# One level of Strassen's scheme in the input products of four SwiGLU layers, with two of the weight sums made by accumulating transfers

## The chip, the core and the metric

The program runs on one core of one Trainium2 chip. The metric is the device time of one execution in microseconds. A core has TensorE (PE), which multiplies a stationary operand of up to 128x128 with a moving one; VectorE (DVE), ScalarE (ACT) and GpSimd (POOL) for the elementwise work; SyncE (SP), which here issues the transfers; and 16 DMA engines. PSUM holds the accumulators of PE, eight banks of 128x512 float32.

## The reference

A trunk of two layers, 512 tokens, width 1024, in float32:

```python
def swiglu(h, w_in, w_out):
    gu = h @ w_in
    a, b = gu[..., :D_FF], gu[..., D_FF:]
    return (jax.nn.silu(a) * b) @ w_out

for l in range(DEPTH):
    x = x + 0.5 * swiglu(rmsnorm(x, norm_ffn1[l]), w_ffn1_in[l], w_ffn1_out[l])
    h = rmsnorm(x, norm_mix[l])
    x = x + mixing_sublayer(h, w_in[l], b_forget[l], ret_norm[l], w_o_ret[l], w_o_fox[l], w_out[l])
    x = x + 0.5 * swiglu(rmsnorm(x, norm_ffn2[l]), w_ffn2_in[l], w_ffn2_out[l])
return rmsnorm(x, norm_final)
```

D_FF is 2816, so each of the four `w_in` has 1024 rows and 5632 columns, 2816 for the gate and 2816 for the up half, 22 tiles of 128 columns each. `mixing_sublayer` (retention, forgetting attention, gates) is not touched by the change but for the buffers that it shares.

## The kernel before

The residual stream lives on chip as eight tiles `x0` to `x7`, features on the partitions and 512 tokens along the free axis. Products are made to float32 accuracy from operands that are rounded to PE's float32r: every operand is split into a rounded part H (a cast on ACT) and the rest L (a subtract on DVE or POOL), and each product is three matmuls, H by H, H by L and L by H (`mm3`, lines L175 to L177; in `proj_tok`, with tokens standing, L194 to L196).

A SwiGLU (`ffn`) runs in two parts of 12 and 10 column tiles (`FF_PARTS`). `ffn_in` takes two tiles of the gate, then two of the up half: `pair` loads a 1 MiB block of weights (`staged`, two staging buffers named `wst`), and `split` makes H and L of each 128x1024 half, in a ring of three buffers `wH` and three `wL`. The weights stand and the tokens move: 8 row tiles by 3 matmuls of 512 columns per column tile, 1056 for an FFN. The result has features on the partitions. DVE multiplies it by R, the inverse norm of every token spread over the partitions (it goes through DRAM for that); ACT makes the silu, POOL the product `u` (L284) and its L part. The output product follows for the part: 24 or 20 blocks of `w_ffn_out`, and DVE adds the result to the residual tile (L324). In the second part `prep` makes H and L of each finished residual tile for the next stage, and its square for the norm. The last SwiGLU (`ffn_last`) makes its output product with tokens standing, and ends with the final norm.

At the start, token tiles `xi` are loaded and turned by PE (`xT`, L825), and 256 KB pieces of the first weights come between them, so that the first product can begin with the first token tile.

A scheduler of the language orders the instructions of each engine and gives them buffers; every engine then runs its list in order. All loads are issued by SP and lie in one queue, in the order of SP's list.

Of the kernel before, what the change touches and what calls it, by code (L numbers as in the profile page):

```python
# [22 lines left out]
FF_PARTS = ((0, 12), (12, 10))  # L23
# [10 lines left out]
    "x": 8, "xh": 16, "v": 8, "o": 8, "y": 8, "g": 6, "r": 3, "qk": 8, "a": 8, "p": 3, "t": 5,  # L34
}
WB = 3
# [3 lines left out]
def trunk(  # L40
# [36 lines left out]

    def wide(name, dt=F32):
        return sp.tile([P, 10 * P], dt, tag="wide", bufs=3, name=name)
# [13 lines left out]
    # ---- constants  # L93
# [3 lines left out]
    gvec = const.tile([P, P], F32, name="gvec")  # L97
    G.memset(gvec, 0.0)
    load(gvec[0:DEPTH * KD], norm_ffn1.rearrange("l (m p) -> (l m) p", p=P))
    gcol = const.tile([P, P], F32, name="gcol")  # L100
    ones = const.tile([P, P], F32, name="ones")
# [5 lines left out]
    # per-feature gains, one column of 128 features each  # L107
    def gain(n, l, m):
        c = (n * DEPTH + l) * KD + m
        return gcol[:, c:c + 1]  # L110

# [4 lines left out]
    def gains(a, b):  # L116
        o = pst("pt", 2, "gT")
        PE.transpose(o[:, 0:P], gvec, ident)
        V.tensor_copy(gcol[:, a:b], o[:, a:b])

    def rest_of_constants():
        for n, v in ((1, norm_mix), (2, norm_ffn2)):
            load(
                gvec[n * DEPTH * KD:(n + 1) * DEPTH * KD, :],
                v.rearrange("l (m p) -> (l m) p", p=P),
            )
        load(gvec[6 * KD:NV, :], ret_norm.rearrange("l (m p) -> (l m) p", p=P))
        gains(DEPTH * KD, NV)
        load(mask, c_mask)
# [5 lines left out]
    # ---- weights: a float32 chunk, split into a rounded part and the rest  # L135
# [7 lines left out]
    def halves(nm, dims, idx):  # L143
        """a pair [128, *dims] of float32r tiles for each index of the loaded chunk"""
# [21 lines left out]
    def pair(nm, parts, nk=KD):  # L166
        """columns of two output tiles: for each, H and L as [128, nk, 128]"""
# [11 lines left out]
    def proj(o, w, mvH, mvL, k0=0, nk=KD, first=True, last=True):  # L179
        """o[128 features, T] (+)= W[:, 128 columns].T @ x over nk row tiles."""  # L180
# [7 lines left out]
    def proj_tok(o, b, w, k0, nk, last_k, mvH, mvL):  # L188
        """o[tokens of block b, 512 columns] += x.T @ W over nk row tiles"""
# [8 lines left out]
    # ---- residual tile done: operands of the next sublayer and its statistics  # L198
    def prep(n, l, m, src=None):
        g = gain(n, l, m)  # L200
        src = xs[m] if src is None else src
        xH[m], xL[m] = st("xh", f"xH{m}", FR), st("xh", f"xL{m}", FR)
# [5 lines left out]
        sq = st("a", f"sq{m}")  # L208
        S.activation(sq, src, AF.Square)  # L209
        if m == 0:  # L210
            sqa[0] = sq
        else:
# [687 lines left out]
```

## Time and profile before

| | us |
|---|---|
| median of 3 runs | 2246.72 (2246.62 to 2247.15) |
| span of the profiled execution | 2244.8 |
| PE busy | 2229.5 (99 %) |
| DVE busy | 1058.3 (47 %) |
| ACT busy | 773.7 (34 %) |
| POOL busy | 579.8 (26 %) |
| chain that ended last | 99 % PE |
| DMA queue of SP | 217.36 MB, 30.6 % of 16 engines |

The busy time of an engine is the time in which at least one of its instructions runs; matmuls overlap each other, so that one shows a duration of 0.39 us where the next starts 0.23 us later. The chain of waits follows the last instruction back to what released it, step by step. Idle time of an engine matters only where that engine, or one that waits for it, is on this chain.

### The profile page before, as it was taken

The numbers are of one execution on the slowest core, as the hardware profiler recorded it, in microseconds if no ns is written. First come the engines' busy times: TensorE is split into PE (matmuls) and PEld (weight loads), VectorE is DVE, ScalarE is ACT, GpSimd is POOL, SyncE is SP. The second block draws the span as 40 slices with busy tenths as digits, with TensorE's granted clock in tenths as the row PEclk, the third lists the DMA queues.
The fourth block names the chain that finished last, engine by engine and source line by source line (L and its number), as shares of the span: only waits on it lengthen the run. The fifth ranks groups of instructions, "written<-read, shape, count | busy, mean of one in ns | idle before, by whom it ended". The sixth has DMA issues, their size and how long they took to land.

```text
span 2244.8 us, 25332 instructions
## 1 busy us (share of the span) xinstructions
PE 2229.5 (99%) x10142; PEld 1850.5 (82%) x10142; DVE 1058.3 (47%) x1452; ACT 773.7 (34%) x1136; POOL 579.8 (26%) x419
## 2 busy tenths in 40 slices
PE   9999999999999999999999999999999999999998
PEld 7888888888878888888888888888888788888887
DVE  4433444557754444344434334446487544433442
ACT  4322233345542332222333223334455333232232
POOL 3220321454221232012232101225532222220121
PEclk9999999999999999999999999999999999999999
DMA  5323224333222332322332232243332233322231
GB/s 159 103 80 117 94 78 125 94 88 115 78 78 94 104 106 81 106 96 80 108 105 98 89 108 94 82 129 90 104 99 76 75 99 118 98 95 94 94 108 61
DMA packets 221557, 218.97 MB, mean 98 GB/s; under 512 B 7040, under 2 KB 205040, under 8 KB 221440
## 3 DMA queue, kind: packets, MB, share of 16 engines
q1 hardware_dynamic: 221440, 217.36, 30.6%
q8 instruction: 79, 1.29, 0.2%
q14 instruction: 38, 0.31, 0.0%
HBM read 215.18 MB, written 2.16 MB: 97 GB/s over the span
## 4 chain that ended last, share of the span: by engine, by line
PE 99%; DVE 0%; SPq 0%; DMA 0%; ACT 0%; issue 0%; POOLq 0%; POOL 0%; ACTq 0%
PE pb L177 7%; PE pb L175 7%; PE pb L176 7%; PE pa L177 7%; PE pa L175 7%; PE pa L176 7%; PE po L176 6%; PE po L177 6%; PE po L175 6%; PE pg L177 3%; PE pg L176 3%; PE pg L175 3%; PE pv L196 1%; PE prq L175 1%; PE pv L195 1%; PE prq L177 1%
## 5 line engine op out<-in xcount | busy, mean ns | idle before, releaser
L284 POOL TENSOR_TENSOR u<-t,sil 128x512 f32<-128x512 f32 x88 | 128.5, 1462 | 876.5 <-DVE t L282 169.8
L175 PE MATMUL po<-uH,wH_o 128*128 128x512 f32 x528 | 205.4, 389 | 0.0
L176 PE MATMUL po<-uL,wH_o 128*128 128x512 f32 x528 | 205.4, 389 | 0.0
L177 PE MATMUL po<-uH,wL_o 128*128 128x512 f32 x528 | 205.4, 389 | 0.0
L282 DVE TENSOR_TENSOR t<-pb,R 128x512 f32<-128x512 f32 x88 | 60.8, 691 | 237.3 <-PE pb L177 236.1
L273 DVE TENSOR_TENSOR t<-pa,R 128x512 f32<-128x512 f32 x88 | 60.5, 691 | 231.8 <-PE pa L177 224.8
L137 ACT CAST wH_o<-wst_o 128x768 fp32r<-128x768 f32 (+1 forms) x96 | 75.3, 785 | 245.4 <-PE po L176 176.9
L138 POOL TENSOR_TENSOR uL<-u,uH 128x512 fp32r<-128x512 f32 x88 | 127.7, 1452 | 62.3 <-ACT uH L137 62.3
L138 DVE TENSOR_TENSOR wL_o<-wst_o,wH_o 128x768 fp32r<-128x768 f32 (+1 forms) x96 | 87.1, 907 | 109.9 <-ACT wH_o L137 100.5
L213 POOL TENSOR_TENSOR sq<-sq,sq 128x512 f32<-128x512 f32 x42 | 65.7, 1565 | 203.8 <-ACT sq L209 203.7
L176 PEld LDWEIGHTS po<-uL,wH_o 128*128 128x128 f32 x528 | 99.1, 188 | 20.8
L177 PEld LDWEIGHTS po<-uH,wL_o 128*128 128x128 f32 x528 | 99.1, 188 | 20.5
L175 PEld LDWEIGHTS po<-uH,wH_o 128*128 128x128 f32 x528 | 99.1, 188 | 20.5
L177 PE MATMUL pg<-xH,wL_g 128*128 128x512 f32 x256 | 100.5, 393 | 0.0
L176 PE MATMUL pg<-xL,wH_g 128*128 128x512 f32 x256 | 100.4, 392 | 0.0
L175 PE MATMUL pg<-xH,wH_g 128*128 128x512 f32 x256 | 100.4, 392 | 0.0
L137 ACT CAST uH<-u 128x512 fp32r<-128x512 f32 x88 | 54.7, 622 | 124.3 <-POOL u L284 124.2
L324 DVE SCALAR_TENSOR_TENSOR x<-po,x 128x512 f32<-128x512 f32 x48 | 33.2, 692 | 90.9 <-PE po L177 90.9
L177 PE MATMUL pa<-xH,wL_f20a 128*128 128x512 f32 x176 | 68.6, 390 | 0.0
L177 PE MATMUL pa<-xH,wL_f11a 128*128 128x512 f32 x176 | 68.6, 390 | 0.0
L177 PE MATMUL pa<-xH,wL_f21a 128*128 128x512 f32 x176 | 68.6, 390 | 0.0
L177 PE MATMUL pb<-xH,wL_f21b 128*128 128x512 f32 x176 | 68.6, 390 | 0.0
(306 smaller groups left out, 6011.8 us busy)
## 6 DMA issues: line engine op xcount, KB each, us to landing
wst_o<-in_w_ffn_out SPq DMA_DIRECT2D x24, 768.0 KB
wst_g<-in_w_in SPq DMA_DIRECT2D x16, 1024.0 KB
wst_o<-in_w_ffn_out SPq DMA_DIRECT2D x24, 640.0 KB
wst_f20a<-in_w_ffn_in SPq DMA_DIRECT2D x11, 1024.0 KB
wst_f20b<-in_w_ffn_in SPq DMA_DIRECT2D x11, 1024.0 KB
wst_f11a<-in_w_ffn_in SPq DMA_DIRECT2D x11, 1024.0 KB
wst_f11b<-in_w_ffn_in SPq DMA_DIRECT2D x11, 1024.0 KB
wst_f21a<-in_w_ffn_in SPq DMA_DIRECT2D x11, 1024.0 KB
```

Source lines behind the costliest of these rows:

```text
L137: S.copy(hi, src)
L138: (lo_eng or V).tensor_tensor(out=lo, in0=src, in1=hi.bitcast(F32), op=ALU.subtract)
L175: PE.matmul(o, wh, mh, start=first, stop=False)
L176: PE.matmul(o, wh, ml, start=False, stop=False)
L177: PE.matmul(o, wl, mh, start=False, stop=last)
L195: PE.matmul(o, mvH[kk][:, bs], lo[:, k], start=False, stop=False)
L196: PE.matmul(o, mvL[kk][:, bs], h[:, k], start=False, stop=kk == last_k)
L213: G.tensor_tensor(out=sqa[0], in0=sqa[0], in1=sq, op=ALU.add)
L273: V.tensor_tensor(out=t, in0=o, in1=R(), op=ALU.mult)
L282: V.tensor_tensor(out=t, in0=o, in1=R(), op=ALU.mult)
L284: G.tensor_tensor(out=u, in0=t, in1=sil[jj], op=ALU.mult)
L324: V.scalar_tensor_tensor(out=xs[m], in0=os_[jj], scalar=0.5, in1=xs[m], op0=ALU.mult, op1=ALU.add,)
```

## The change

Strassen's scheme, in Winograd's form, splits a product of two matrices into quarters and makes seven products of quarters for eight. Here the tokens are cut into two halves of 256, the 1024 rows of the weights into two halves of 512, and the columns into gate and up. Of a group of column tiles the four weight blocks are A11 and A12 (the gate's upper and lower rows) and, of the up half, S1's first summand (upper rows) and A22 (lower rows). Line by line:

- `FF_PARTS` names three parts of two groups; a group has four column tiles, but one of each FFN has two.
- `prep_forms` takes the place of `prep` ahead of an FFN. From residual tiles k and k+4 it makes the seven forms of the tokens: scaled tiles (`b2`, `n1`), and four sums `m1` to `m4` of half tiles, each split into H and L.
- `ffn_group` loads seven blocks of 512 rows: A12, A11 and A22 plainly; S1 (the sum of the up half's upper and lower rows) and S3 (the sum of the gate's and the up half's upper rows) each by a plain load of one summand and a second transfer, issued by POOL, that adds the other to it in the buffer (`summed`). Two more sums, S1+A11 and S1+A11+A12, are made by DVE (`more`). The buffers swap roles between even and odd groups. Seven steps follow, each 24 matmuls in which a 128-token form stands and 512 columns of weights move (256 in the group of two tiles).
- The accumulators now have tokens on the partitions: the norm is a scalar per partition, `u` is made by ACT and DVE, and `turned` brings it back by 22 x 4 transposes per FFN, for the output product.
- Weight rings get a fourth place from the tag `y`. Output blocks are 1 MiB (768 KB in the last part). `ffn` may finish residual tiles in pairs (k, k+4).
- At the start all token tiles are loaded first, in the order 4, 0 (the loop over `i` starts at tile 4, and `prep_forms` runs from tile 0 on).

```diff
-FF_PARTS = ((0, 12), (12, 10))
+FF_PARTS = (((0, 4), (4, 4)), ((8, 4), (12, 4)), ((16, 2), (18, 4)))
...
+    def prep_forms(n, l, k, stat=True):
...
+        scaled(b2[:, 0:T], b2[:, T:2 * T], x2, gain(n, l, k + 4))
...
+        scaled(n1[:, 0:H2], n1[:, H2:T], x1[:, 0:H2], ngain(n, l, k))
+        b1 = st("t", "b1")
+        S.activation(b1, x1, AF.Copy, scale=gain(n, l, k))
...
+        V.tensor_tensor(out=m1, in0=b1[:, 0:H2], in1=b1[:, H2:T], op=ALU.subtract)
...
+        split(mt, mh, ml)
...
+            square(x1, k == 0)
+            square(x2, False)
...
+    def wtile(w, i):
+
+        tag = w if i % 4 else "y"
...
+        def summed(ts, r0, c0, r1, c1):
+            for s, t in enumerate(ts):
+                load(v3(t), piece(r0, c0, s))
+                G.dma_start(v3(t), piece(r1, c1, s), accum_op=ALU.add)
+            return ts
+
+        K2 = 4 * P
+        raw = {}
+        raw["A12"] = plain(small_tiles("qk", "A12_") if odd else big_tile("A12_"), K2, ca)
+        raw["A11"] = plain(small_tiles("qk", "A11_") if odd else big_tile("A11_"), 0, ca)
+        raw["S1"] = summed(small_tiles("v", "S1_"), 0, cb, K2, cb)
+        raw["S3"] = summed(small_tiles("v", "S3_"), 0, ca, 0, cb)
+        raw["A22"] = plain(big_tile("A22_") if odd else small_tiles("qk", "A22_"), K2, cb)
...
+        def step(nm, form, banks, first):
+            wh = weights(nm)
+            for q in range(2):
+                o = banks[q][:, 0:cw]
+                for k in range(4):
+                    h, lo = (x[:, k % nk] for x in wh[k // nk])
+                    sh, sl = forms[form, k, q]
+                    mm(o, sh, h, start=first and k == 0, stop=False)
+                    mm(o, sh, lo, start=False, stop=False)
+                    mm(o, sl, h, start=False, stop=k == 3)
...
+        Y = [acc("Y0"), pst("po", 1, "Y1")]
+        step("A12", "b21", Y, True)
+        X = [acc("X0"), acc("X1")]
+        step("A11", "n11", X, True)
...
+            S.copy(c1[q], X[q][:, 0:cw])
+            V.tensor_tensor(out=c1[q], in0=Y[q][:, 0:cw], in1=c1[q], op=ALU.subtract)
+            S.activation(c1[q], c1[q], AF.Silu, scale=r[:, q:q + 1])
+        more("S1", "A11", "A11")
+        step("S1A11", "m2", X, False)
...
+        step("S1", "m1", W, True)
+        step("S3", "m3", X, False)
...
+        more("S1A11", "A12", "A12")
+        step("S1A11A12", "b22", W, False)
...
+        step("A22", "m4", X, False)
...
+    def turned(ub, j, u):
+
+        o = pst("pt", 2, "uT")
+        for b in range(TB):
+            PE.transpose(o[:, b * P:(b + 1) * P], ub[b][:, j * P:(j + 1) * P], ident)
...
-        if m % 2 == 0:
-            first_weights(m // 2)
...
+        if m < 4:
+            prep_forms(0, 0, m)
```

The order of the instructions shows the change at three places. First ACT at the start of the program. `w0H` is a cast of a 256 KB weight piece, `xH` the token tile's rounded part, `sq` a square. Before:

```order
L137 CAST w0H_98<-w0_96 128x512
L203 ACTIVATE xH0_113<-xT_108,gcol_77 128x512
L137 CAST w0H_104<-w0_102 128x512
L209 ACTIVATE sq0_117<-xT_108 128x512
L137 CAST w0H_139<-w0_137 128x512
L203 ACTIVATE xH1_127<-xT_122,gcol_77 128x512
L137 CAST w0H_145<-w0_143 128x512
```

And now, from its 20th operation on, up to the cast that PE's first product waits for (`wH_0`, from A12's first half; `mh` are casts of the four sums):

```order
L152 CAST wH_2_307<-wst_A11_0_252 128x1024
L152 CAST mh0_149<-mt_144 128x1024
L152 CAST wH_3_311<-wst_A11_0_252 128x1024
L152 CAST mh2_209<-mt_204 128x1024
L244 ACTIVATE b2_1_166<-x5_86,gcol_74 128x512
L152 CAST mh1_178<-mt_173 128x1024
L244 ACTIVATE b2_3_227<-x7_88,gcol_74 128x512
L244 ACTIVATE b2_2_196<-x6_87,gcol_74 128x512
L152 CAST mh3_239<-mt_234 128x1024
L152 CAST wH_0_273<-wst_A12_0_249 128x1024
```

Weight casts stood between the token tiles; now all forms of the tokens, and casts of three other weight blocks, stand ahead of `wH_0`.

Second, SP's list in the first FFN. Before, at the end of the first part's input product (`wst_f10a` and `wst_f10b` are gate and up blocks, `wst_o10` output blocks):

```order
L91 DMA wst_f10b8_902<-in_w_ffn1_in 128x8x256
L91 DMA wst_f10a10_978<-in_w_ffn1_in 128x8x256
L91 DMA wst_f10b10_1046<-in_w_ffn1_in 128x8x256
L91 DMA wst_o10_0_0_0_1131<-in_w_ffn1_out 128x6x256
L91 DMA wst_o10_0_0_1_1177<-in_w_ffn1_out 128x6x256
L91 DMA wst_o10_0_2_0_1227<-in_w_ffn1_out 128x6x256
```

Now, at the change from the first part to the second (groups 8 and 12; a row stands for a load, `x2` for both halves of a block; POOL's adding transfers into S1 and S3 are in POOL's list):

```order
L100 DMA wst_o10_0_3_1089<-in_w_ffn1_out 128x8x256
L100 DMA wst_A12_8_1149<-in_w_ffn1_in 128x2x512 x2
L100 DMA wst_A11_8_1152<-in_w_ffn1_in 128x2x512 x2
L100 DMA wst_A22_12_1449<-in_w_ffn1_in 128x2x512 x2
L100 DMA S1_12_0_1437<-in_w_ffn1_in 128x2x512
L100 DMA S1_12_1_1438<-in_w_ffn1_in 128x2x512
L100 DMA S3_12_0_1443<-in_w_ffn1_in 128x2x512
L100 DMA S3_12_1_1444<-in_w_ffn1_in 128x2x512
L100 DMA wst_o10_8_0_1748<-in_w_ffn1_out 128x8x256
L100 DMA A11_12_0_1433<-in_w_ffn1_in 128x2x512
L100 DMA A11_12_1_1434<-in_w_ffn1_in 128x2x512
```

Blocks of an odd group's seven loads now stand in a row, with an output block ahead of A11.

Third, DVE around the change from group 8 to group 12. Before, in the same product, a split of weights and a product with R take turns (`t2` for the up half):

```order
L138 TENSOR_TENSOR wL_f10a61_697<-wst_f10a6_690,wH_f10a61_696 128x1024
L282 TENSOR_TENSOR t2_682<-pb_657,R_302 128x512
L138 TENSOR_TENSOR wL_f10b60_761<-wst_f10b6_758,wH_f10b60_760 128x1024
L273 TENSOR_TENSOR t1_725<-pa_700,R_302 128x512
L138 TENSOR_TENSOR wL_f10b61_765<-wst_f10b6_758,wH_f10b61_764 128x1024
```

Now (`wL_44` is A11's first half, `wL_42` and `wL_43` A12's; the third row of this piece adds S1 to A11):

```order
L444 TENSOR_TENSOR d_1280<-W0_1283,d_1280 128x512
L446 SCALAR_TENSOR_TENSOR d_1280<-e0_1349,rsx_345,d_1280 128x512
L153 TENSOR_TENSOR wL_44_1489<-A11_12_0_1433,wH_44_1488 128x1024
L409 TENSOR_TENSOR A11_12_0_1433<-S1_12_0_1437,A11_12_0_1433 128x1024
L153 TENSOR_TENSOR wL_42_1455<-A12_12_0_1429,wH_42_1454 128x1024
L444 TENSOR_TENSOR d_1280<-W1_1284,d_1280 128x512
L452 SCALAR_TENSOR_TENSOR c1_1239<-X0_1205,rsx_345,c1_1239 128x512
L153 TENSOR_TENSOR wL_43_1459<-A12_12_1_1430,wH_43_1458 128x1024
L409 TENSOR_TENSOR A12_12_0_1429<-A11_12_0_1433,A12_12_0_1429 128x1024
L452 SCALAR_TENSOR_TENSOR c1_1239<-X1_1206,rsx_345,c1_1239 128x512
```

The split of A11's first half and the sum S1+A11 stand ahead of A12's split and of the last operations of the group before.

## Rows read from the trace of the kernel before

**Rows 1.** Page: span, busy time, share and instructions of every engine, granted clock in tenths.

```profile
span 2244.8 us, 25332 instructions
PE 2229.5 (99%) x10142; PEld 1850.5 (82%) x10142; DVE 1058.3 (47%) x1452; ACT 773.7 (34%) x1136; POOL 579.8 (26%) x419
PEclk9999999999999999999999999999999999999999
```

**Rows 2.** Page: the chain of waits by engine.

```profile
PE 99%; DVE 0%; SPq 0%; DMA 0%; ACT 0%; issue 0%; POOLq 0%; POOL 0%; ACTq 0%
```

**Rows 3.** Timeline, PE, in the last product: start, duration, line, operation, shape.

```profile
2225.41 0.39 PE L195 MATMUL pz<-ozL,uH 128*128 128x512 f32 x1
...
2230.40 0.39 PE L196 MATMUL pz<-ozH,uL 128*128 128x512 f32 x1
2230.62 0.28 PE L194 MATMUL pz<-ozH,uH 128*128 128x256 f32 x1
...
2237.70 0.28 PE L196 MATMUL pz<-ozH,uL 128*128 128x256 f32 x1
```

**Rows 4.** Chain of waits, transposes of the mix: start, duration, what, count.

```profile
599.27 0.79 PE ptr L591 x7
```

**Rows 5.** Windows: start:end, length, busy time (count) by engine, clock, DMA share, GB/s.

```profile
0.00:381.75 381.75, 376.29 (x1665) 310.33 (x1665) 161.31 (x172) 122.72 (x162) 86.72 (x66) 1.00 0.34 108
771.60:1131.75 360.15, 360.15 (x1597) 298.20 (x1595) 146.68 (x146) 108.20 (x138) 75.04 (x52) 1.00 0.30 98
```

**Rows 6.** Timeline, all engines, start of the program.

```profile
0.72 1.28 ACT L137 ACT_TABLE_LOAD   x1 [0.72 <-PEq L884]
6.50 1.22 PE L175 MATMUL pa<-xH,w0H 128*128 128x512 f32 x2 [1.02 <-ACT xH L203]
```

**Rows 7.** Chain of waits, end of the program.

```profile
2238.01 0.44 DVE xt L356
2240.47 0.72 ACT xt L412
```

**Rows 8.** Lines, ACT: out<-in, shapes, count, busy us, mean ns, idle before.

```profile
L203 ACT ACTIVATE xH<-x,gcol 128x512 fp32r<-128x512 f32 x40 | 28.8, 721 | 5.4 <-DVE x L324 3.6 <-DVE x L794 1.8
L209 ACT ACTIVATE sq<-x 128x512 f32<-128x512 f32 x40 | 24.5, 617 | 0.0
L137 ACT CAST wH_f20a<-wst_f20a 128x1024 fp32r<-128x1024 f32 x22 | 23.2, 1053 | 81.8 <-PE pb L176 34.8 <-issue 34.4 <-PE po L176 6.3
```

**Rows 9.** Lines, DVE, and one tile's minimum, median and maximum in ns.

```profile
L273 DVE TENSOR_TENSOR t<-pa,R 128x512 f32<-128x512 f32 x88 | 60.5, 691 | 231.8 <-PE pa L177 224.8 <-DMA R<-r_d 6.9
L138 DVE TENSOR_TENSOR wL_f20a<-wst_f20a,wH_f20a 128x1024 fp32r<-128x1024 f32 x22 | 34.9, 1585 | 11.2 <-ACT wH_f20a L137 9.9
L138 DVE TENSOR_TENSOR wL_rv<-wst_rv,wH_rv 128x1024 fp32r<-128x1024 f32 x8 | 9.8, 1225 | 14.1 <-ACT wH_rv L137 14.1
L138 DVE TENSOR_TENSOR wL_f20a<-wst_f20a,wH_f20a x22: 1215/1226/2362, 753.7 to 1043.2; 128x1024 fp32r<-128x1024 f32 x22
```

**Rows 10.** Windows with the load queue full.

```profile
3.00:20.00 17.00, 14.46 (x63) 10.87 (x64) 11.86 (x19) 11.22 (x20) 4.98 (x4) 1.00 1.09 317
48.50:49.50 1.00, 1.00 (x6) 0.84 (x5) 0.00 (x0) 0.29 (x1) 1.00 (x2) 1.00 1.09 388
```

**Rows 11.** Timeline, one output weight block: SP's issue, and ACT's first use of it.

```profile
2158.19 33.61 SPq L91 DMA_DIRECT2D wst_oz<-in_w_ffn_out  x6
2163.24 1.15 ACT L137 CAST ozH<-wst_oz 128x512 fp32r<-128x512 f32 x2 [0.91 <-DMA wst_oz<-in_w_ffn_out]
```

**Rows 12.** Page: DMA queues, packets, megabytes, share of 16 engines; no other queue has entries.

```profile
q1 hardware_dynamic: 221440, 217.36, 30.6%
q8 instruction: 79, 1.29, 0.2%
q14 instruction: 38, 0.31, 0.0%
```

More of the change, by code (lines that the diff above doesn't have):

```diff
@@ L114, in rgain, with gains @@
         return gcol[:, c:c + 1]
-    def gains(a, b):
+    def gains(a, b, parts):
+        gvec = st("t", "gvec")[:, 0:P]
+        G.memset(gvec, 0.0)
+        for r, v in parts:
+            v = v.rearrange("l (m p) -> (l m) p", p=P)
+            load(gvec[r:r + v.shape[0]], v)
         o = pst("pt", 2, "gT")
@@ L119, in gains @@
         V.tensor_copy(gcol[:, a:b], o[:, a:b])
+        V.tensor_scalar(
+            out=ncol[:, a:b], in0=o[:, a:b], scalar1=-1.0, scalar2=None, op0=ALU.mult
+        )
     def rest_of_constants():
[L122 to L128, printed above, removed]
+        gains(DEPTH * KD, NV, (
+            (DEPTH * KD, norm_mix), (2 * DEPTH * KD, norm_ffn2), (6 * KD, ret_norm),
+        ))
         load(mask, c_mask)
@@ L352, in turn @@
                     S.copy(xt[b][n], o)
+            for n in range(2):
+                g = st("x", f"gf{n}")
+                load(
+                    g, norm_final[n * T:(n + 1) * T].rearrange("(o d) -> o d", o=1).to_broadcast([P, T])
+                )
+                gf.append(g)
         def add(b, n, o, c0=0, c1=T):
@@ new lines, in ffn_last, with product @@
+        for pi, groups in enumerate(FF_PARTS):
+            last = pi == len(FF_PARTS) - 1
+            u, todo = ffn_in(rtok, w_i[l], groups)
+            f0, nf = groups[0][0], sum(n for _, n in groups)
+            def product(o, b, unit, c0=0, c1=T):
+                k, h, lo = unit
+                bs = slice(b * P, (b + 1) * P)
+                for i in range(2):
+                    uh, ul = (x[:, bs] for x in u[k + i])
+                    hh, ll = h[:, i, c0:c1], lo[:, i, c0:c1]
+                    PE.matmul(o, uh, hh, start=k + i == 0, stop=False)
+                    PE.matmul(o, uh, ll, start=False, stop=False)
+                    PE.matmul(o, ul, hh, start=False, stop=k + i == nf - 1)
+            if pi == 0:
+                turn()
+            for n in range(2):
+                if last and n == 1:
+                    break
+                os_ = [acc(f"po{b}", b % 2 == n) for b in range(TB)]
+                for unit in units(f0, nf, n):
+                    if todo:
+                        todo.pop(0)()
+                    for b in range(TB):
+                        product(os_[b], b, unit)
+                for b in range(TB):
+                    if last:
+                        added(b, 0, os_[b])
+                    else:
+                        add(b, n, os_[b])
```

421 lines of the change are left out of this document (251 added, 170 removed).

## The prediction

> **What bounds the kernel now.** I read the page's shares first. TensorE (PE) is busy 2229.5 of 2244.8 us at a granted clock in the top tenth, VectorE (DVE) 47 % [rows 1], and the chain that ended last is 99 % PE [rows 2]. So the time is the number of matmuls times their pitch, and a change gains only if it takes matmuls away without starving PE. The pitch comes from consecutive starts in the timeline: 22 steps of 512 columns from 2225.41 to 2230.40 are 4.99 us, 0.2267 us each; 59 steps of 256 columns from 2230.62 to 2237.70 are 0.120 us each [rows 3]. Seven 128-column transposes take 0.79 us, 0.113 each [rows 4]. The stage table tells what PE loses at either end: a period from one layer's FFN to the next stage is 360.15 us, all of it PE [rows 5]. It holds 1584 matmuls of 512 columns, 359.1 us, so the product runs at its pitch. The first period lasts 381.75 us, and holds 35 matmuls of 512 columns and 34 transposes more (11.8 us); so the prologue loses 381.75 - 360.15 - 11.8 = 9.8 us. It begins its first product at 6.50, as soon as a quarter-megabyte weight piece and one token tile are there [rows 6]. The last product ends at 2238, and a 7 us chain follows that the change leaves alone [rows 7].
>
> **Matmuls taken away and added.** Each of the four FFNs' input products goes from 1056 matmuls of 512 columns to 840 of 512 and 168 of 256 (its fifth group is two tiles wide), and since its result now has tokens on the partitions, 88 transposes of 128 columns bring it back. In the order of the whole program 512-column matmuls fall by 852, 256-column ones rise by 648 (864 and 672 in the input products; the last output product, in other parts, has 12 more of 512 and 24 fewer of 256), 128-column ones by 353. In time: -852 x 0.2267 = -193.2, +648 x 0.120 = +77.8, +353 x 0.113 = +39.9: **-75.5 us** of PE work. Here weights move and token forms stand, as in the last product, whose pitch is the one quoted [rows 3]; so both ends of this cost lie close (0.11 to 0.13 for the 256-column step: 71 to 84).
>
> **Cover on DVE and ScalarE (ACT).** A four-tile group is 168 matmuls and 16 transposes, 39.9 us of PE. DVE has 14 weight splits and four sums of weight blocks of 128x1024, at 1.225 us where GpSimd (POOL) rests and 1.585 in the mean beside POOL, up to 2.362 [rows 9], and some 14 operations of 128x512 at 0.69 [rows 9]: 18 x 1.225 + 9.7 = 31.7 us. ACT has 14 casts at 1.053 and a dozen smaller ones [rows 8], 23 us. Both fit. POOL's arithmetic leaves the FFN (the 88 products u and their low parts), so I take DVE's lower price and cost these operations at nothing.
>
> **Prologue.** Before, weights and token tiles alternate in the queue. Now all 2 MB of tokens come first, and the first group needs forms made of two token tiles. The order shows the stall: PE's first product takes weight block wH_0, and ACT casts that block as its 29th operation, after 11 activations of token forms (0.721, four of them half as wide, which I put at 0.45 between 0.36 and 0.72), 8 squares (0.617) and 7 casts (1.053) [rows 8]; with its own cast 20.2 us. ACT can begin them when a second token tile has been copied, near 8.5 us at the 317 GB/s of the first loads [rows 10]. So the first product starts near 28.7 us, against 6.50, and a first silu behind it stalls PE for some 1.6 more (its table load of 1.28 [rows 6] stands ahead of the next weight cast; the rest is an estimate). Of these 30.3 us, 4.6 are transposes and token sums that PE does anyway. Lost: 25.7 against 9.8, **+15.9** (11 to 22, by whether ACT's list runs without gaps or the forms come in pairs).
>
> **Starts of the other three FFNs.** Forms need two residual tiles and a chain of five DVE operations behind the last sum, where one cast and one subtract did before. At 0.69 each this is about 1 to 2 us beyond what the order lets PE do meanwhile: **+4** (0 to 8).
>
> **The weight queue.** This is the large unknown. All loads share one hardware queue, in order [rows 12], at 388 GB/s [rows 10]; on average there is room (98 GB/s [rows 5], and a group would want 7 MiB in 39.9 us, 184). The burst matters. In the second group of a part, SP's list holds A22, S1, S3, a 1 MiB output block and only then A11, and A22 waits until the group before has split its sixth block, 24.3 us after that group's start (107 matmuls). From there 4.5 MiB stand ahead of A11's first half: 2.0 us to start and 12.1 us at 388 GB/s, so it lands at 38.4. (A 1 MiB block issued at 2158.19 was in use at 2163.24 [rows 11]: 5.05 us for 2.7 us of bytes and ACT's own wait, hence the 2.0.) The group before ends at 168 x 0.2267 = 38.1. Beside these, POOL issues four accumulating loads of 0.5 MiB each; the trace of before has none [rows 12]. Free of cost, they leave 38.4; sharing the engines by bytes they push it to 43.8 (2.1 MB at 388 is 5.4); at twice the price to 49.2. I take two thirds of a fair share, 42.0, since each one starts only when its plain half is there and POOL has issued it. What this costs hangs on the order in which ACT and DVE wait. In the first FFN they take A11's first half ahead of A12, both engines queue everything behind it, and PE runs dry 33.65 us after the group's start: 8.35 lost, in each of 2 groups. In the second they take it second: it is needed at 37.6, 4.4 lost, twice. In the two FFNs of the second layer A12 goes first and it is needed at 41.3: 0.7, four times. Sum 28.3; **+28**, between 11 (38.4) and 86 (49.2). These places are estimates from the order's rows and the durations above.
>
> A page speaks against this part. The Trainium skill, "DMA: Bandwidth & Descriptors" (Queues, rings and completion order), says each DMA engine takes turns between its queues, a packet at a time; by that rule a second queue gains no bandwidth, and the sum would stand at 43.8, 12 us above mine. No row of before shows two busy queues.
>
> **The second output block.** It stands behind 4 MiB of the next group's blocks and their accumulating loads, and would land between 40 and 50 us where it is needed at 44.4; 0 to 6 us in each of eight places. I take 1 us: **+8** (0 to 40).
>
> **The sum.** -75.5 + 15.9 + 4 + 28 + 8 = -19.6. The profiled span was 2244.8, the runs' median 2246.72, 1.9 more; so 2225.2 for a profiled execution and **2227.1** for the median. Covers at nothing: the output products hide the last transposes of a part (they run between output products of earlier tiles); the statistics' trip to DRAM falls away but was hidden.
>
> **Rivals.**
> 1. Accumulating loads nearly free (A11 lands at 38.4, output block 3): -75.5 + 15.9 + 4 + 11 + 3 = -41.6, 2205.1. For it: DMA is busy 30.6 % [rows 12]. Against it: the burst is back to back at full rate.
> 2. Slower than before: an accumulating load costs twice its bytes. Its place is the second group of a part, its price 7.2 us per group more than mine (49.2 against 42.0), and the output blocks then lose 30: -75.5 + 15.9 + 4 + 86 + 30 = +60.4, 2307.1. It decides from where those two terms together pass 55.6, a landing near 44. For it: such a load must read what it adds to. The Trainium skill, "Collectives: The Full Stack" (The bandwidth ceiling), puts an add in the DMA at half the copy rate because of its two source reads; no run here shows that yet.
> 3. DVE becomes the bound. If half its wide operations meet POOL's descriptor work as they met POOL's arithmetic (1.79, the mean of 1.225 and 2.362 [rows 9]), a group takes 18 x 1.79 + 9.7 = 41.9 against 39.9, 2 us in each of 20 groups: +40 on the forecast, 2267. It decides from 1.68 on. Against it: in this stretch POOL has nothing but issues.
> 4. The queue hides all of it and the prologue too: 2246.7 - 75.5 = 2171. Against it: ACT's list at the start.
>
> **How the numbers follow.** Chances: forecast 0.45 (2210 to 2248), rival 1 0.20 (2187 to 2210), rival 2 0.18 (2257 to 2327), rival 3 0.10 (2242 to 2287), rival 4 0.07. A difference of 0.2 % (4.5 us) is about what a measurement of this kernel can tell from none. Faster: 0.36 of the forecast, rivals 1 and 4, 0.63, rounded down to 0.62; within 0.2 %: 0.07, the forecast's upper edge and rival 3's lower; slower: rival 2, most of rival 3 and the forecast's last bit, 0.31. The range 2187 to 2303 leaves out rival 4 and a good half of rival 2, some 0.17.
>
> **What would show it.** Right: PE's first product near 28 us; PE busy about 2155 us; idle PE ahead of A11's products, ended by a DMA, in the second groups of the first FFN (about 8 us each), less in the later ones; DVE's wide operations near 1.23; accumulating loads that take 1 to 2 times a plain load. Wrong: no idle before A11's or the output block's products (rival 1), idle of 10 us and more in every second group (rival 2), or DVE waited for with wide operations above 1.68 (rival 3). A 512-column pitch above 0.2267 with tokens standing would break the first term.

## The result: 0.58 % slower, and the profile after

The changed kernel takes 2259.61 us in the median (2258.28 to 2261.18), the kernel before 2246.67: a ratio of 1.0058, with a 95 % interval of 1.0044 to 1.0072. The forecast was 2227.1. The profiled execution has a span of 2259.3 us, 14.5 more than the one of before. The page of the changed kernel, first busy times and granted clock (as [rows 1]), then the queues ([rows 12]) and the chain ([rows 2]):

```profile
span 2259.3 us, 26447 instructions
...
PE 2180.2 (96%) x10286; PEld 1812.3 (80%) x10286; DVE 1410.9 (62%) x1896; ACT 994.8 (44%) x1414; POOL 432.0 (19%) x332
...
PEclk6999999999999999999989999999999999999999
...
q1 hardware_dynamic: 205440, 239.38, 33.7%
q0 software_dynamic: 25984, 46.14, 11.7%
...
PE 89%; DMA 5%; DVE 4%; ACT 1%; issue 1%; SPq 0%; POOL 0%; POOLq 0%; ACTq 0%; DVEq 0%
```

PE is busy 49 us less than before, not 75.5 (a product at a lower clock, and the first one behind a stop, are busy for longer). It stands idle for 4 % of the span, and two of the forty slices show a lower granted clock: the first, and the one in which layer 1 starts (1130 to 1186 us). In the chain, DMA, DVE and ACT now hold 10 %. A queue that was not there before, POOL's, takes 11.7 % of the DMA engines.

The waits of PE's instructions, summed by who ended them (line and tile, releaser, us in all, times, the longest):

```profile
PE xs L315 <- POOL sq L220: 17.3, 1, 17.3
PE Y L394 <- ACT wH L152: 13.4, 4, 9.6
PE X L394 <- ACT wH L152: 7.7, 5, 2.4
PE Y L394 <- DVE wL L153: 7.4, 5, 2.0
...
PE po L190 <- DVE o L153: 4.9, 2, 2.5
```

One wait of 17.3 us is for POOL's squares, 14 waits of 28.5 us together for the high and low parts of weights (`wH`, `wL`), and two are for a split in the mix stages (`po`). The waits alone don't tell what to mend, since what released PE had waited itself.

The matmuls themselves cost what was assumed. In the chain of waits, 22 steps of 512 columns with tokens standing take 4.99 us, 0.2267 each, and 24 of 256 columns 2.88, 0.120 each:

```profile
66.50 4.99 PE W L394 x22
...
309.37 2.88 PE X L394 x24
```

So the loss can be laid out by place: in each stretch, the distance from one matmul's start to the next, less the nominal pitch of its width (0.2267, 0.120, 0.113), summed. That counts idle time and slower clock alike. Worked out from the starts in the two traces, in us ("predicted more" are the terms of the prediction's sum):

| place | before | after | predicted more | more |
|---|---|---|---|---|
| start of the program (to 62.7 us after, to 32 before) | 6.7 | 40.5 | 15.9 | 33.8 |
| second groups (A11) | 0 | 15.8 | 28 | 15.8 |
| starts of the other three FFNs | 0 | 24.8 | 4 | 24.8 |
| mix stages | 10.9 | 16.8 | 0 | 5.9 |
| output blocks and the rest | 0 | 8.7 | 8 | 8.7 |
| tail | 7.1 | 7.3 | 0 | 0.2 |
| sum | 24.7 | 113.9 | 56 | 89.2 |

89.2 less the 75.5 of matmuls saved is +13.7, against 14.5 between the spans. The prediction had 56 in place of the 89.2; that is its whole error of some 33 us. Three lines carry the loss: the program's start, the other starts, and the second groups.

**The start.** PE in the timeline of the changed kernel (start, duration, line, operation, idle time before it and its releaser), and a window of that stretch (length, busy time and count of PE, PEld, DVE, ACT, POOL, granted clock, DMA share, GB/s):

```profile
13.47 0.63 PE L1037 MATMUL xT<-ident,xi 128*128 128x128 f32 x4 [1.49 <-DMA xi<-in_x]
31.39 1.87 PE L315 MATMUL xs<-ones,sq 128*128 128x1 f32 x8 [17.30 <-POOL sq L220]
42.90 1.22 PE L394 MATMUL Y<-wH,b 128*128 128x512 f32 x2 [9.63 <-ACT wH L152]
...
44.34 0.63 PE L394 MATMUL X<-wL,n 128*128 128x512 f32 x1
44.77 1.05 PE L394 MATMUL X<-wH,n 128*128 128x512 f32 x2
```

```profile
14.80:48.90 34.10, 7.87 (x22) 6.53 (x23) 32.87 (x34) 14.68 (x21) 15.01 (x12) 0.50 0.77 202
```

The first product stands at 42.90, not at 28.7, against 6.50 in [rows 6]. PE has next to nothing to do from 14.1 us on, and in the stretch from 14.8 to 48.9 us its granted clock is 0.5, the 1.2 GHz level; the first products start 0.43 us apart (44.34 and 44.77), not 0.23. The lower level is there again behind smaller stops of PE, for instance in these two stretches:

```profile
60.00:62.00 2.00, 2.00 (x6) 1.54 (x6) 2.00 (x3) 1.02 (x2) 0.00 (x0) 0.50 0.77 210
1156.00:1165.00 9.00, 4.58 (x15) 3.35 (x15) 7.89 (x12) 1.99 (x2) 3.08 (x2) 0.50 0.00 0
```

An estimate from the starts in the trace: 56 products of 512 columns stand 0.38 to 0.48 us ahead of the next one with no idle time between, most of them 0.43, where the kernel before has 7. At 0.2 us more each, the lower clock is some 10 of the 89.2 us.

Why the first product comes so late is seen on three engines. ACT's first form of half width, its three waits for DVE and the cast that the product takes; DVE's sums `mt` of 256 columns; POOL beside them:

```profile
11.46 0.51 ACT L244 ACTIVATE n<-x,ncol 128x256 fp32r<-128x256 f32 x1 [4.44 <-DVE x L1038]
...
22.30 1.04 ACT L152 CAST mh<-mt 128x1024 fp32r<-128x1024 f32 x1 [0.64 <-DVE mt L274]
...
28.05 1.04 ACT L152 CAST mh<-mt 128x1024 fp32r<-128x1024 f32 x1 [3.76 <-DVE mt L274]
...
40.85 1.04 ACT L152 CAST mh<-mt 128x1024 fp32r<-128x1024 f32 x1 [8.97 <-DVE mt L274]
41.81 1.04 ACT L152 CAST wH<-wst_A 128x1024 fp32r<-128x1024 f32 x1
```

```profile
13.18 0.42 DVE L266 TENSOR_TENSOR mt<-b 128x256 f32<-128x256 f32 x1
...
16.77 1.49 DVE L266 TENSOR_TENSOR mt<-b 128x256 f32<-128x256 f32 x1
...
40.35 0.47 DVE L274 SCALAR_TENSOR_TENSOR mt<-x,gcol,mt 128x256 f32<-128x256 f32 x1
```

```profile
15.30 4.08 POOL L220 TENSOR_TENSOR sq<-sq 128x512 f32<-128x512 f32 x3 [0.18 <-ACT sq L216]
```

ACT, whose list I had added up, is idle for 8.97 us ahead of its last cast of a sum: it waits for DVE. From 11.46 us to the end of `wH` at 42.85 it waits 13.4 us in all, each time for DVE, and works 18.0. DVE works without a gap from 12.8 to 40.8 us, and a sum of 256 columns that takes 0.42 us at 13.18 takes 1.49 at 16.77, while POOL adds squares, and 0.47 again at 40.35.

**A second group**, at 205 to 217 us: SP's issue of A11, ACT's cast of its first half, PE's first product:

```profile
204.93 2.18 SPq L100 DMA_DIRECT2D A<-in_w_ffn_in  x2
```

```profile
215.00 3.88 ACT L152 CAST wH<-A 128x1024 fp32r<-128x1024 f32 x4 [6.92 <-DMA A<-in_w_ffn_in]
```

```profile
217.05 0.73 PE L394 MATMUL Y<-wH,b 128*128 128x512 f32 x2 [2.29 <-ACT wH L152]
```

A11 was issued at 204.93, as soon as its buffer was free, and was in use at 215.00: 10 us for 0.5 MiB, with the output block (issued at 200.82) and two adding transfers (issued at 200.77 and 204.88) beside it.

**The start of layer 1's first FFN**, where 14.8 us are lost between 1140 and 1170:

```profile
1155.61 0.79 PE L394 MATMUL Y<-wH,b 128*128 128x512 f32 x1 [2.36 <-ACT b L244]
...
1164.82 1.22 PE L394 MATMUL X<-wH,n 128*128 128x512 f32 x2 [2.40 <-ACT wH L152]
```

```profile
1154.51 1.49 DVE L245 SCALAR_TENSOR_TENSOR n<-x,ncol,n 128x256 fp32r<-128x256 f32 x1
...
1157.35 0.47 DVE L270 SCALAR_TENSOR_TENSOR mt<-x,ncol,b 128x256 f32<-128x256 f32 x1
```

```profile
1153.62 3.52 POOL L220 TENSOR_TENSOR sq<-sq 128x512 f32<-128x512 f32 x2 [5.37 <-ACT sq L216]
```

PE waits for forms (`b`) and weights in turn; DVE has no idle time from 1140 to 1162.8 us, and again its 256-column operations take 1.49 us beside POOL's additions and 0.47 a moment later.

### The profile page after: what moved, and what is told of

Read it like the earlier page. It is cut to its first block, busy times and chain, and to the rows that moved or that the text cites. A ratio compares the mean times of both kernels' runs of the same rounds, so it can differ in the third digit from the quotient of the medians.

```text
span 2259.3 us, 26447 instructions
## 1 busy us (share of the span) xinstructions
PE 2180.2 (96%) x10286; PEld 1812.3 (80%) x10286; DVE 1410.9 (62%) x1896; ACT 994.8 (44%) x1414; POOL 432.0 (19%) x332
## 3 DMA queue, kind: packets, MB, share of 16 engines
q0 software_dynamic: 25984, 46.14, 11.7%
## 4 chain that ended last, share of the span: by engine, by line
PE 89%; DMA 5%; DVE 4%; ACT 1%; issue 1%; SPq 0%; POOL 0%; POOLq 0%; ACTq 0%; DVEq 0%
PE X L394 19%; PE W L394 9%; PE po L191 6%; PE po L190 5%; PE po L192 5%; PE Y L394 4%; DMA A<-in_w_ffn_in 3%; PE pg L192 3%; PE pg L190 3%; PE pg L191 3%; PE uT L462 2%; PE po L622 2%; PE po L621 2%; PE po L620 2%; PE pv L210 1%; PE prq L190 1%
## 5 line engine op out<-in xcount | busy, mean ns | idle before, releaser
L394 PE MATMUL X<-wH,mh 128*128 128x512 f32 (+1 forms) x576 | 209.4, 375 | 6.8 <-ACT wH L152 5.3
L394 PE MATMUL X<-wL,mh 128*128 128x512 f32 (+1 forms) x576 | 214.8, 373 | 0.2 <-DVE wL L153 0.2
L394 PE MATMUL X<-wH,ml 128*128 128x512 f32 (+1 forms) x576 | 214.5, 372 | 0.0
L153 DVE TENSOR_TENSOR wL<-A,wH 128x1024 fp32r<-128x1024 f32 x116 | 141.2, 1222 | 76.9 <-ACT wH L152 76.2
L152 ACT CAST wH<-wst_A 128x1024 fp32r<-128x1024 f32 x104 | 109.1, 1051 | 165.3 <-PE po L191 56.0
L153 DVE TENSOR_TENSOR wL<-wst_A,wH 128x1024 fp32r<-128x1024 f32 x104 | 126.6, 1223 | 87.8 <-ACT wH L152 86.7
L152 ACT CAST wH<-A 128x1024 fp32r<-128x1024 f32 x116 | 120.7, 1052 | 111.3 <-DVE A L409 31.0
L394 PE MATMUL Y<-wH,b 128*128 128x512 f32 (+1 forms) x384 | 119.0, 382 | 18.4 <-ACT wH L152 13.4
L394 PE MATMUL X<-wH,n 128*128 128x512 f32 (+1 forms) x384 | 118.8, 383 | 2.4 <-ACT wH L152 2.4
L394 PE MATMUL W<-wH,b 128*128 128x512 f32 (+1 forms) x384 | 117.4, 372 | 0.0
```

The costliest lines, as they stand in the source:

```text
L152: S.copy(hi, src)
L153: (lo_eng or V).tensor_tensor(out=lo, in0=src, in1=hi.bitcast(F32), op=ALU.subtract)
L394: PE.matmul(*args, skip_group_check=True, **kw)
```

## The experiments

All changes are against the changed kernel unless said. Losses by place are counted as in the table above; "25.0 for 15.8" means 25.0 in this run and 15.8 in the changed kernel. The theory that they test: DVE's list, stretched by POOL's additions of squares, sets the starts, and the adding transfers delay A11. The rival is the prediction's own reading: ACT's list sets the program's start, and a second queue costs by its bytes.

**POOL's additions left out.** The squares are still made; the norm then comes from one tile alone.

```diff
-            square(x1, k == 0)
-            square(x2, False)
+            for src in (x1, x2):
+                sq = st("a", "sq")
+                S.activation(sq, src, AF.Square)
+                if src is x1 and k == 0:
+                    sqa[0] = sq
```

> Left out: in the forms of the tokens ahead of each of the four FFNs, GpSimd's seven additions of squares (the squares themselves are still made, the norm then comes from one tile alone). Theory A (these additions slow DVE's operations beside them, in the changed kernel's start from 0.47 to about 1.5 us per 256 columns, and DVE's list sets the start of every FFN): the first FFN product comes near 32 us instead of 42.9, the start of layer 1's first FFN loses about 7 us less, and the time falls by 15 to 25 us, to 2235 to 2245. Rival B (ACT's list is what sets the start, as the prediction had it): the first product stays within 3 us of 42.9 and the time within 5 us of 2259.6. Rival C (the squares' sum itself, on which the token sums wait until 31.4 us, is what holds PE): the gap of 17 us ahead of the token sums goes, but the first product still stands near 42.

Measured: 2241.98 us, 0.9980 of before (0.9971 to 0.9990), 17.6 less than the changed kernel. PE's first product, ACT's wait ahead of it, DVE's operations, and POOL's issues of transfers beside them:

```profile
32.34 1.22 PE L397 MATMUL Y<-wH,b 128*128 128x512 f32 x2 [18.13 <-ACT wH L152]
```

```profile
30.30 1.04 ACT L152 CAST mh<-mt 128x1024 fp32r<-128x1024 f32 x1 [3.71 <-DVE mt L274]
```

```profile
14.98 0.41 DVE L266 TENSOR_TENSOR mt<-b 128x256 f32<-128x256 f32 x1
...
18.53 0.48 DVE L274 SCALAR_TENSOR_TENSOR mt<-x,gcol,mt 128x256 f32<-128x256 f32 x1
```

```profile
18.40 3.89 POOL L376 DMA_DIRECT2D S<-in_w_ffn_in  x3 [2.13 <-DMA S<-in_w_ffn_in]
```

The first product comes 10.6 us earlier, and the sums stay at 0.41 to 0.48 us, also beside POOL's issues of the adding transfers: it is POOL's additions that stretch them. ACT still waits for DVE. By place: the program's start loses 27.5 for 40.5, layer 1's first FFN 8.7 for 14.8, layer 1's second 1.8 for 5.8; the start of layer 0's second FFN did not gain, and the second groups gave 9 back (25.0 for 15.8), with another order in DVE's list. Theory A holds; under rival C, the squares' sum itself, the product would have stayed near 42.

**Copies on ACT at the program's start**, and **both together**.

```diff
-        V.tensor_copy(xs[m], o)
+        S.copy(xs[m], o)
```

> Only at the start of the program: the eight copies of the turned token tiles (0.69 us each) go from DVE to ACT. Theory A (DVE's list is what sets the first product): it comes 4 to 6 us earlier than 42.9, and the time falls by 3 to 6 us, to about 2255. Rival B (ACT's list sets it, as predicted): 4 to 5 us later, about 2264.

Measured: 2253.35 us, 1.0032 of before (1.0022 to 1.0042), 6.3 less than the changed kernel, and the first product at 36.91:

```profile
36.91 1.22 PE L394 MATMUL Y<-wH,b 128*128 128x512 f32 x2 [2.24 <-ACT wH L152]
```

Work that was taken from DVE and put onto ACT made the start shorter, so ACT's list was not its bound. The gain was just over the 3 to 6 us expected.

> Left out again: GpSimd's additions of squares ahead of the FFNs; and the eight copies of the turned token tiles go from DVE to ACT. Theory A (DVE's list, stretched by GpSimd, was the bound of the start, and behind it lies ACT's own list, which the prediction put at 28.7 us with the copies on DVE and some 4.6 more with them): the first product at 29 to 33 us, no earlier than the 32.3 of the run without the additions by more than 3 us, since ACT's list now is as long as DVE's. Rival B (DVE is still the bound): 26 to 28 us.

Measured in a single run, from which only the places are read: 2242.64 us, and the first product at 29.42. ACT's list from its sixth copy on:

```profile
29.42 1.22 PE L397 MATMUL Y<-wH,b 128*128 128x512 f32 x2 [15.32 <-ACT wH L152]
```

```profile
10.21 0.59 ACT L1041 COPY x<-xT 128x512 f32<-128x512 f32 x1 [0.28 <-PE xT L1040]
...
28.33 1.04 ACT L152 CAST wH<-wst_A 128x1024 fp32r<-128x1024 f32 x1
```

From 10.21 to 29.4 ACT runs without a gap. Only here, with DVE relieved twice, is it the bound. That it ends so near the 28.7 of the prediction is in part luck: this list holds eight copies more than the predicted one, and the expectation had reckoned 4.6 us for them.

**The transfers copy and don't add.**

```diff
-                G.dma_start(v3(t), piece(r1, c1, s), accum_op=ALU.add)
+                G.dma_start(v3(t), piece(r1, c1, s))
```

> Left out: the 88 transfers that GpSimd issues copy instead of adding (same number, bytes, queue and waits; S1 and S3 then hold one summand). Theory A (the add costs the DMA engines 1.8 times a copy's time: in the changed kernel the GpSimd queue takes 11.7 % of the engines' time for 46.1 MB, the SP queue 33.7 % for 239.4 MB): that queue's share falls to about 6.5 %, a transfer of it lands in 6 us instead of 9.4, and the waits for A11 in the second groups, 15 us in all in the first two FFNs, fall to 5 to 10; the time falls by 5 to 12 us. Rival B (a second queue and GpSimd's issue cost the same with or without an add): share and waits stay, the time stays within 3 us of 2259.6.

Measured: 2232.60 us, 0.9935 of before (0.9919 to 0.9952), 27 less than the changed kernel. The page's line of POOL's queue, SP's issue of the same A11 as above, and ACT's first use of it:

```profile
q0 software_dynamic: 12672, 46.14, 6.0%
```

```profile
198.62 2.18 SPq L100 DMA_DIRECT2D A<-in_w_ffn_in  x2
```

```profile
205.97 3.89 ACT L152 CAST wH<-A 128x1024 fp32r<-128x1024 f32 x4 [4.20 <-DMA A<-in_w_ffn_in]
```

The same 46.14 MB take 6.0 % of the engines' time in 2232.3 us for 11.7 % in 2259.3, in 12672 packets for 25984: an add costs 1.97 copies. A11 is in use 7.4 us after its issue, not 10.1. The second groups lose 3.8 us for 15.8. The gain was more than the 5 to 12 us expected, since the program's start gained 4, layer 1's second start 5, and one output block 4 as well. In the two traces every engine's instructions and all issues stand in the same order, so the 27 us belong to the add and not to a new order.

**No second transfers at all** (the line left out).

> Left out: the 88 adding transfers altogether. Theory A (they share the load queue's bandwidth, and so delay A11's blocks): the waits for A11 in the second groups of the first two FFNs, 15 us in all, go to under 3, the start of the second FFN loses 3 us less, and the time falls by 15 to 20 us, to about 2242. Rival B (A11 is late because its buffer comes free late, when the group before has split its last block at 204.9 in the profile, and the 1 MiB output block stands ahead of it): more than half of the waits stay, and the time falls by under 8 us. Under both the start of the program stays near 42.9 us to the first product, if DVE's list is what holds it, or moves to under 38 if GpSimd's waits for these transfers do.

Measured: 2232.17 us, 0.9936 of before (0.9921 to 0.9950), more of a gain than the 15 to 20 us expected. The second groups lose 0.7 us in all; in the one shown above, A11 is again issued 28 us after the group before began, but is in use 4.2 us later, not 10.1:

```profile
197.35 19.98 SPq L100 DMA_DIRECT2D A<-in_w_ffn_in  x4
```

```profile
201.56 1.05 ACT L152 CAST wH<-A 128x1024 fp32r<-128x1024 f32 x1 [1.04 <-PE X L393]
```

Together with the run before: the add costs the 27 us, and the copies that remain cost nothing in the total (2232.6 against 2232.2). At their place they do cost: A11 comes 3 us later than without them, and the second groups lose 3.8 against 0.7 us. In this run the starts lose a little more instead, with another order in DVE's list, so the total doesn't tell the copies' own price. The first product stays at 42.22, so it isn't these transfers that hold it.

**The first FFN as before** (its functions, prologue and parts put back for layer 0's first FFN, the other three as changed).

> The first FFN of layer 0 and the start of the program are those of the kernel before; the other three FFNs are those of the changed kernel. Theory A (the changed kernel's loss sits in the start of the program, 33.9 us more than before, and in the first FFN's second groups, 9.9; a later FFN is worth about 18.9 us of PE work less what its start costs): 2259.6 - 33.9 - 9.9 + 18.9 = 2235, 2230 to 2241, faster than both kernels. Rival B (the loss is spread over all four FFNs, and what the first FFN loses is made good elsewhere): within 5 us of 2255.

Measured: 2251.42 us, 1.0019 of before (1.0010 to 1.0029), 8.2 less than the changed kernel and not 25. The start loses 5.2 us as it should, but the second FFN takes over the ills: its start and second groups lose 25.7 for 10.0, layer 1's first FFN 22.5 for 15.7. Waits of PE:

```profile
PE Y L394 <- ACT wH L152: 8.5, 3, 3.8
PE xs L315 <- POOL sq L220: 6.8, 2, 5.9
```

Theory A failed, and rival B had the number (within 5 us of 2255): what the first FFN lost is now lost elsewhere. What an FFN loses is not its own property: with other work ahead, the scheduler chose another order (in the second FFN fewer than half of DVE's and of ACT's operations stand in the same sequence as in the changed kernel), and the second FFN's groups got the long waits for A11 that the first had.

**S1 and S3 made by DVE.** S1's loaded summand is the up half's upper block, its other is A22, and S3 is A11 plus the same summand; all are on chip.

```diff
-        raw["S1"] = summed(small_tiles("v", "S1_"), 0, cb, K2, cb)
-        raw["S3"] = summed(small_tiles("v", "S3_"), 0, ca, 0, cb)
+        raw["S1"] = plain(small_tiles("v", "S1_"), 0, cb)
+        raw["S3"] = small_tiles("v", "S3_")
...
+        for s in range(nh):
+            V.tensor_tensor(out=raw["S3"][s], in0=raw["A11"][s], in1=raw["S1"][s], op=ALU.add)
+            V.tensor_tensor(out=raw["S1"][s], in0=raw["S1"][s], in1=raw["A22"][s], op=ALU.add)
         more("S1", "A11", "A11")
```

> No transfer adds: S1 is made by DVE from its loaded summand and A22, S3 from A11 and that same summand, all three on chip already, so a group loads 4 MiB instead of 7 and DVE has four more operations of 1.225 us per group (88 in all, 108 us). Theory A (the adding transfers cost 27 us, as the copy in their place showed, and DVE has room for the sums except at the starts of the FFNs): 2236 to 2248, the waits for A11 gone, the first product 3 to 6 us later than 42.9. Rival B (DVE at 36.6 of 39.9 us per group becomes the bound): waits for DVE in every group, 2255 or more.

Measured: 2255.66 us, 1.0044 of before (1.0027 to 1.0061). The second groups lose 3.8 us, as without the adds; but the starts lose 40.2, 6.7, 19.5 and 10.5 for 40.5, 4.2, 14.8 and 5.8. The first product stands at 46.0, as expected; the time is rival B's (2255 or more), but not by its waits in every group. Against the copying run, there are 22 us more at the four starts, where DVE was full, and nothing inside the groups, though DVE is now busy for 67 % of the span. DVE's and ACT's lists come in another order as well, and the two causes were not tried apart.

**Both: the first FFN as before, and the sums on DVE.**

Both changes above, in one kernel.

> The first FFN and the program's start as in the kernel before, and in the other three FFNs S1 and S3 made by DVE from blocks on chip, no transfer adds. Theory A (what was left of the loss with the first FFN as before, 2251.4, lies in the waits for adding transfers in the second FFN's start and second groups, some 25 us, and in the starts): 2222 to 2236, faster than before by 0.5 to 1 %. Rival B (DVE is the bound once it makes all the sums): 2245 or more.

Measured: 2245.96 us, 0.9997 of before (0.9987 to 1.0006): no difference, where theory A had 2222 to 2236. The second FFN's groups lose 2.8 for the 15.1 of the run with the first FFN as before, and the three starts together 41.9: the starts took most of what the groups gained.

**Squares summed by PE**, on top of that.

```diff
-            square(x1, k == 0)
-            square(x2, False)
...
+            for i, src in enumerate((x1, x2)):
+                sq = st("a", "sq")
+                S.activation(sq, src, AF.Square)
+                for b in range(TB):
+                    PE.matmul(
+                        sqp[0][:, b:b + 1], sq[:, b * P:(b + 1) * P], ones,
...
```

> As the kernel with the first FFN as before and S1 and S3 made by DVE, and besides, ahead of the other three FFNs the squares of the eight token tiles are summed by PE (eight times four matmuls of one column, accumulated, some 3.3 us of PE per FFN) and not by seven GpSimd additions. Theory A (what is left of the loss, some 40 us at the three starts, comes from DVE's list there, and GpSimd's additions stretch it): DVE's 256-column operations at the starts fall from 1.5 to 0.47 us, the starts lose 3 to 6 us less each, PE's extra matmuls partly lie in its idle time, and the time falls to 2232 to 2242, faster than before. Rival B (DVE's list is as long without them, or PE now waits in order for the last squares): 2244 to 2252.

Measured: 2247.14 us, 1.0002 of before (0.9993 to 1.0011). (What its matmuls leave in the accumulator is not the full sum of squares; their number and size are those of the full sum.) The three starts lose 24.2 us for the 41.9 of the run before, and all places together 18.6 less; but the time stays, because each one-column product of float32 is two instructions in the trace, and 84 more of them at 2 x 0.113 are 19.0 us of PE. One of DVE's sums in the whole program, in this kernel and in the one without PE's squares (busy us, mean of one in ns):

```profile
L268 DVE SCALAR_TENSOR_TENSOR mt<-x,gcol,mt 128x256 f32<-128x256 f32 x12 | 5.8, 479 | 0.1
```

```profile
L267 DVE SCALAR_TENSOR_TENSOR mt<-x,gcol,mt 128x256 f32<-128x256 f32 x12 | 11.9, 995 | 0.1
```

So POOL's additions cost these three starts some 18 us here too, and PE's squares cost as much.

**The same sums in one pass, and later.** Squares rounded to float32r, two columns wide, made behind the forms:

```diff
+    def late_stats():
+        o = pst("pt", 2, "xs")
+        for m in range(KD):
+            sq = st("a", "sq", FR)
+            S.activation(sq, xs[m], AF.Square)
...
+            for b in range(TB):
+                PE.matmul(
+                    o[:, 2 * b:2 * b + 2], sq[:, b * P:(b + 1) * P], ones_r,
...
-        rtok = lazy(lambda: rstd(sqa[0], D, "x"))
+        rtok = lazy(late_stats)
```

> As the kernel with the first FFN as before and S1 and S3 made by DVE (2246.0), with the squares of the other three FFNs summed by PE in float32r, in one pass where float32 takes two, and only behind the forms in the order of the program. In the kernel before this one the starts lost 18.5 us less, and PE's 84 extra one-column products, two passes each, took it back. Theory A (the gain at the starts stays, and the price halves): 2234 to 2241, faster than before by 0.25 to 0.5 %. Rival B (squares that come later hold PE in order at the first silu or ahead of the first product): 2244 or more.

Measured: 2239.33 us (2238.80 to 2241.12), 0.9969 of before (0.9958 to 0.9981): faster than both kernels, by 0.3 % against the one before. Its page:

```profile
span 2237.3 us, 26094 instructions
...
PE 2196.2 (98%) x10322; PEld 1829.8 (82%) x10322; DVE 1370.9 (61%) x1854; ACT 941.3 (42%) x1349; POOL 356.3 (16%) x269
```

Three FFNs by Strassen's scheme save 56.6 us of matmuls; the starts still lose 26.3 and the mix stages some 6 more than before. The one pass and the later place were not tried apart; 96 instructions fewer at 0.113 us are 10.8 us by themselves, and the starts lose no less than the 24.2 of the run before, so no gain of the later place is seen.

## Why the prediction was wrong, step by step

- **Matmuls saved, -75.5: right.** The pitch held with tokens standing, for 512 and 256 columns, wherever the granted clock was at its upper level. The sum has no term for the lower one, which is some 10 us by the estimate above.
- **The program's start, +15.9: wrong, 33.8.** The step that failed is the choice of ACT's list as the one that sets the first product. I added ACT's operations and never DVE's, which at the same place holds eight copies, all L parts, four sums per pair of tiles and the weight splits. The trace shows DVE without a gap to 40.8 us and ACT waiting for it; the run with more work on ACT was faster; and with DVE relieved twice the product came at 29.42, against 28.7 worked out for ACT. So the sum for ACT was about right (18.0 us of work from 11.46 us on in the trace, against 20.2 from 8.5 on: 29.5 and 28.7, two errors that cancel in part), but it was not the bound. Of the 17.9 us that this term missed, 14.2 are the later product, and 3.1 come from the start of before, which I had put at 9.8 and which is 6.7 by the table's count.
- **DVE's lower price, taken because POOL's arithmetic leaves the FFN: wrong at the starts.** It leaves the groups, where weight splits took 1.22 us, but the seven additions of squares stand exactly where the forms are made. [rows 9] had the price, 1.225 alone and up to 2.362 beside POOL, and rival 3 used it, but for the groups. Leaving the additions out gave 17.6 us. The Trainium skill, "SBUF — State Buffer" (Who interferes with whom), says that a DVE instruction with two inputs in SBUF contends with a GpSimd instruction that reads SBUF, and calls the shared ports an exclusive lock. The trace agrees: 0.42 and 1.49 us above, beside POOL additions of 1.3 to 2.7 us (median 1.56).
- **The other starts, +4: wrong, 24.8.** I counted a chain of five operations behind the last tile. It is a matter of load: a pair of residual tiles gives PE 8.2 us (36 products of 0.2267), and DVE 4.2 us of forms, 1.4 of sums and 1.9 of weight splits at their lower prices, 7.5; with POOL's additions beside them DVE would fall behind pair by pair, and PE would meet the debt at the start. The run without the additions bears this out for layer 1 (8.7 for 14.8 and 1.8 for 5.8) and not for layer 0's second FFN, whose 4.2 us stayed.
- **The weight queue, +28: the place and the pattern right, the path and the size not, 15.8.** As predicted, the first FFN's second groups lost most (3.5 and 6.5), the second's less (5.8 in both), layer 1's next to nothing. But I had one burst begin at 24.3 us, with A11 at its end. In the trace A22 and the summands go out from 7.9 us after the group's start on, and A11 is issued at 28.2, when its own buffer is free; the output block and the adding transfers then hold it for 10 us. It was in use 38.3 us after the group before began (176.7 to 215.0), where I had 42.0. An adding transfer, which I had put between one and two copies, cost 1.97. The Trainium skill, "Collectives: The Full Stack" (The bandwidth ceiling), which I had set beside rival 2, puts the adding step of a collective at half the rate of a copy, for its two source reads; the 1.97 here agrees with the half. Rival 2 was right in its price and wrong in its effect: the second groups lost 15.8 and not 86. The Trainium skill, "DMA: Bandwidth & Descriptors" (Queues, rings and completion order), also set beside this part, has each DMA engine take turns between its queues. By that, copies would delay A11 as well. The runs agree at that place (A11 in use 7.4 us after its issue beside copies, 4.2 without), but the total did not show it. By the prediction's own places a landing at 43.8 would add 14 us, not the 12 that it gives.
- **Output blocks, +8: the number near, by luck.** With the rest it is 8.7, but only 4.3 of it lie at an output block, one of the last FFN (2105 to 2130 us), and not 1 us at each of eight.
- **Mix stages, 0: wrong, 5.9.** Not touched by the change, but ordered anew: in both layers PE waits 2.4 us for DVE's split of the attention's output, which stands behind a weight split in DVE's list. That this is the scheduler's order alone was not tried.
- **Rival 3** (DVE becomes the bound) had the right engine and the wrong place: a group's 168 products hide DVE's work, even with four more sums per group, and the starts don't. The measured time lies in its range and in rival 2's, but not by the waits that either gave.

What stays open: why the same FFN code loses 10 us or 26 in the second FFN according to what stands ahead of it. The runs show that the order changes, not which rule of the scheduler's brings it. The starts were not brought down to nothing in any run, so what is left there (26.3 us at three starts) is open as well.

## To carry to other kernels

When a change adds elementwise work ahead of a product, add up every engine's list at that place, not only the one that makes the last operand; and price each operation by what the neighbouring engines do there, not by its mean over the program. A transfer that adds cost two copies here: count it so wherever loads come in bursts, and look whether its summands are on chip anyway, and whether the engine that would add them has room where they are needed. Savings on the engine that is the bound were kept inside long stretches and lost at their starts: here 18.9 us of matmuls per FFN against 4 to 34 us per start. And a stop of the engine costs more than its length where the products behind it run at the lower clock.

## What the runs showed of the hardware

- An adding transfer into the chip's memory took 1.97 times the DMA engines' time of a copy of the same bytes (11.7 % of 2259.3 us and 6.0 % of 2232.3 for 46.14 MB) and 2.05 times the packets.
- Copies of those bytes in a second queue beside the first cost nothing in the total (2232.6 and 2232.2 us), but in one second group a 0.5 MiB load of the first queue was in use 7.4 us after its issue beside them, 4.2 without any, and 10.1 beside adds.
- A DVE operation of 128x256 with two inputs on chip took 0.41 to 0.48 us alone and beside POOL's issues of transfers, and 1.49 beside POOL's additions of 128x512.
- PE had next to nothing to do from 14.1 to 42.9 us; from 14.8 to 48.9 its granted clock was 0.50, the 1.2 GHz level, and the products in the last six of these us cost about 3 us more than at the upper level.
- A one-column float32 product of 128 rows is two instructions in the trace (192 for 96 products); in float32r, with two columns, it is one (96 for 96).
